# Six conditioning blocks of the second layer summed on ScalarE, GpSimd and VectorE for one column

## The chip, the cores and the metric

The kernel runs on one core of a Trainium2 chip. The metric is the device time of one execution in microseconds (us). Besides DMA the core has TensorE (PE in the rows; its weight loads are PEld), VectorE (DVE), ScalarE (ACT), GpSimd (POOL) and SyncE (SP), which here only issues DMAs. Each engine works through its own instructions in the order in which the program holds them.

## The reference, cut to what matters

Two layers of a trunk act on 256 latent and 256 context tokens of 1024 channels. Each layer is conditioned: a vector of 6 x 1024 numbers, for the latents and for the context apart, gives a shift, a scale and a gate to the token mixing and to the channel mixer.

```python
for l in range(DEPTH):                                  # DEPTH = 2
    last = l == DEPTH - 1
    mod = silu(c) @ w_mod[l] + b_mod[l]                 # (1024) x (1024, 6144)
    mod_c = silu(c_ctx) @ w_mod[l] + b_mod[l]
    sh1, sc1, g1, sh2, sc2, g2 = split(mod, 6)
    csh1, csc1, cg1, csh2, csc2, cg2 = split(mod_c, 6)
    h = modulate(rmsnorm(x, norm_mix[l]), sh1, sc1)
    hc = modulate(rmsnorm(xc, norm_mix[l]), csh1, csc1)
    mix, mix_c, v_pair = token_mixers(h, hc, ...)       # attention, RWKV-7, spatial gating
    x = x + g1 * mix
    h = modulate(rmsnorm(x, norm_ffn[l]), sh2, sc2)
    x = x + g2 * swiglu(h, w1, w3, w2)
    if not last:
        ...                                             # the same for the context, with cg1, csh2, csc2, cg2
return x                                                # the latents alone
```

In the last layer csh2, csc2 and cg2 are used by nothing.

## The kernel before

The work of a layer is: `phase_ab` (all projections of the token mixers, the recurrence, attention, spatial gating), `phase_m` (merge of the branches and output projection) and `phase_f` (channel mixer). Weights come in tiles of 128 x 1024 (512 KB) through SP into the tag `wr` (`wtile`, line 153), which in the second layer's `phase_ab` has three buffers. ScalarE rounds each half (`wh`, line 124), VectorE or, for the gates, GpSimd forms the rest (`wl`, line 125), and three products per 128 channels restore the precision. The results of all projections, of the conditioning and of its transposes share two PSUM buffers, the tag `mm`.

`phase_ab` is made of threads: K (projections of a pair of heads, `rps`), P (`psc`, `pvs`, `pbk`), I (inverse of triangular blocks, mostly on VectorE, `itp` and `it` at lines 629 and 630), C (the recurrence, `cw`, `cu`, `cn`, `py`), Q (its output norm), A and T (attention, `ptm`, `pt`, `po`), S (spatial gating), G (24 gate projections, `gps`, evicted by ScalarE into `gth` at line 362 and stored to `gate_d` at line 363) and X, the conditioning. `slots` sets the order in which their steps are emitted; a scheduler then puts the instructions of every engine in an order by priority and by when it takes buffers to be free. C, I and P have high priority, X and G have none.

The 12 conditioning blocks of a layer are 512 columns of `w_mod` each. `mod` computes a block for both columns (latents and context) on TensorE: the four quarters of 256 rows are loaded in turn (line 243, 512 KB each), and each quarter gives eight products of the 128 x 32 stationary `cr[:, k]` with 128 columns of weights into the PSUM tile `mps` (line 246).

```python
for k in range(2):
    for g in range(4):
        mm(ps[32*g:32*g+32], cr[:, 2*q+k], w[:, 512*k+128*g:512*k+128*g+128],
           start=q+k == 0, stop=q+k == 4)
```

So a block has 32 products and keeps its PSUM tile from the first to the copy in `spread`. `spread` (line 224) copies the rows to the SBUF tile `modr` on ScalarE (line 227), transposes it on TensorE (`mpt`, line 229), and VectorE adds the bias into `modv` (line 230). `mod_v` (line 252) does the same for both columns on the vector engines, and is used in the first layer's `phase_f`: products with a column of `cr` on VectorE and ScalarE (lines 264 to 270), sums on VectorE and GpSimd (`macc`, lines 266 and 271), and at the end products with the selectors `sel` that bring the sum over the partitions (`mvp`, line 276).

The blocks run as follows. First layer: 0 to 3 before `phase_ab`, 4 to 8 as thread X of `phase_ab`, 9 in `phase_m`, 10 and 11 by `mod_v` in `phase_f`. Second layer: 0 to 5 by `mod_v` in the first layer's `phase_f`, and 6 to 11 by `mod` as thread X of the second layer's `phase_ab` (`m1`, line 1142). Blocks 6 to 11 are the shift, scale and gate of the channel mixer; the results of `m1` are taken up after `phase_ab`.

Of the kernel before, what the change touches and what calls it, by code (L numbers as in the profile page):

```python
# [7 lines left out]
F32 = mybir.dt.float32  # L8
# [6 lines left out]
PSUM = bass.MemoryType.PSUM  # L15
# [30 lines left out]
def slots(p):  # L46
    """the order in which the stages of the time mixing are emitted: by a time given to each"""
# [38 lines left out]
def trunk(ctx: ExitStack, tc: tile.TileContext, out, a):  # L86
# [3 lines left out]
    def dm(cl, l, *args, **kw):  # L90
        """a product of a dense class: in the order of the program with the others of the classes in DENSE"""
        r = mm(*args, **kw)  # L92
        if cl in DENSE:
            tc.stamp_issue_order_token(r.ins, f"dense{l}")
        return r
# [31 lines left out]
    def rsqrt(pool, out, x, scale, bias, tag):  # L127
        """out = 1 / sqrt(scale * x + bias): a first guess from the bits, three steps of Newton's method"""
# [10 lines left out]
    class Wt:  # L139
        """a block of weights in two halves of 512 columns, each split into its two parts"""  # L140
# [27 lines left out]
    # conditioning  # L168
# [25 lines left out]
    def params2(L):  # L194
# [11 lines left out]
        # time-mixing vectors  # L206
# [17 lines left out]
    def spread(L, j, ps):  # L224
        """rows 32 g + i of ps to column i of the vectors of block j"""
        r = gp.tile([128, 128], F32, tag="modr", name="modr")
# [6 lines left out]
    def mod(L, js, pool=None, nb=2):  # L233
        """conditioning blocks of 512 columns, 128 to each group of 32 rows of the product; a generator that stops after every quarter of a block"""
# [17 lines left out]
    def mod_v(L, js, pool, share):  # L252
        """the same on the vector engines; a generator that stops after every quarter of a block"""
# [24 lines left out]

    def run(gen, n=None):
# [13 lines left out]
    class Norm:  # L293
        """of x [128, KT, 512], into hh and hl: the squares of each 128 channels, then the rest"""
# [51 lines left out]
    def proj(ps, w, ts_, kt=KT, cl=None, l=0):  # L346
        """feature-major: ps [128, n] = w^T h"""
# [17 lines left out]
    def phase_ab(L, extra):  # L365
        """the three branches up to what the merge takes, as threads whose stages are emitted in the order of slots()"""
# [6 lines left out]
        with tc.tile_pool(name="pb", bufs=1, reuse_waits="tile", side="right") as pb, tc.tile_pool(name="pe", bufs=1, reuse_waits="tile") as pe, tc.tile_pool(name="pbp", bufs=1, space=PSUM, reuse_waits="tile") as pbp:  # L373
# [16 lines left out]
            def conv(ps, w, y, streams):  # L390
                """y [128, ns*256] from ps, zero padded in each stream"""
# [14 lines left out]
            def rnorm(sq, n, scale, bias, name):  # L406
                """1/sqrt(scale * sum over the head + bias), token-major and spread over the head"""
# [12 lines left out]
            def rnorm2(rx, n, name):  # L420
                """the same, feature-major, in PSUM"""
# [14 lines left out]
            if last:  # L436
                # value residual: low rank part
# [24 lines left out]
            def t_common(hp):  # L462
                """one pair of heads: projections, removal key, rates, bonus"""
# [53 lines left out]
            def dirs(ap, d):  # L517
                """[128, 256] of one stream as [128, 4, 64] in the order of processing"""
# [717 lines left out]
```

## Time and profile before

| what | value |
|---|---|
| time, median of 3 runs | 2234.27 us |
| the three runs | 2232.68, 2237.18, 2234.27 us |
| profiled execution, from its first to its last instruction (its span; the page has no other time of it) | 2235.2 us |
| busy: PE, DVE, ACT, POOL | 93%, 60%, 38%, 22% of the span |
| TensorE clock granted, mean | 0.891 |
| second layer's `phase_ab`, its part with conditioning | 1420 to 1840 us |

A busy share counts time in which an engine has an instruction under way; matmuls are pipelined and their ends are modelled, so that a busy TensorE need not be a full one. The chain of work that ended last follows the program back from its last instruction, at each step to what released it: a microsecond on the chain is one that the end waited for. fp32 products appear as two records each.

### The profile page before, as it was taken

The page shows a single profiled execution, that of the slowest core. Times are in us where ns is not written, and L with a number is a line of the kernel's source. Part 1 is how long each engine was busy: PE and PEld are TensorE (multiplying, and loading weights), DVE is VectorE, ACT ScalarE, POOL GpSimd, SP SyncE. Part 2 cuts the span into 40 slices and gives each one's busy share as a digit, 9 for nine tenths or more (in the row PEclk, how much of TensorE's full clock was granted, in tenths as well). Part 3 has the DMA queues.
Part 4 walks back from the last instruction along what each step waited for, and adds up shares of the span by engine and source line. Part 5 has one row for each costly group of instructions (what it writes and reads, how often), then busy time and mean ns, then how long its engine had stood idle before and what let it go on. Part 6 is the DMA issues. An engine that isn't in the chain of part 4 may idle for free.

```text
span 2235.2 us, 36124 instructions
## 1 busy us (share of the span) xinstructions
PE 2075.2 (93%) x13738; PEld 1627.7 (73%) x13738; DVE 1332.0 (60%) x3383; ACT 856.1 (38%) x1776; POOL 498.1 (22%) x589
## 2 busy tenths in 40 slices
PE   4989999899999989898999988899999999988999
PEld 3867666566666668787888867776766667878999
DVE  3576568456367235576753356675876667177665
ACT  3442233443233432354342334432433344245554
POOL 3131132222222223032210002414241333330000
PEclk8997689987878999999999989785997888699999
DMA  7222113221111286245542222311212121375553
GB/s 259 86 72 72 57 34 101 71 69 41 54 44 37 68 319 197 86 150 165 175 145 95 78 90 85 96 58 48 82 61 70 61 88 59 99 256 174 186 181 114
DMA packets 97738, 239.24 MB, mean 107 GB/s; under 512 B 9594, under 2 KB 25594, under 8 KB 97436
## 3 DMA queue, kind: packets, MB, share of 16 engines
q1 hardware_dynamic: 90012, 225.39, 30.7%
q10 hardware_dynamic: 6912, 9.44, 1.2%
q8 instruction: 108, 1.77, 0.3%
q0 software_dynamic: 640, 2.10, 0.3%
q14 instruction: 66, 0.54, 0.1%
HBM read 219.59 MB, written 17.30 MB: 106 GB/s over the span
## 4 chain that ended last, share of the span: by engine, by line
PE 75%; DVE 12%; DMA 4%; issue 3%; ACT 3%; POOL 3%; SPq 0%; ACTq 0%; POOLq 0%; DVEq 0%
PE fps L92 16%; PE gps L92 8%; PE rps L92 6%; PE psc L579 3%; PE yps L1074 3%; PE yps L1075 3%; PE yps L1076 3%; PE mps L246 2%; PE sc L845 2%; DVE it L630 2%; PE pvs L590 2%; DMA mr<-in_w_mod 2%; PE cu L698 1%; DVE itp L629 1%; PE py L686 1%
## 5 line engine op out<-in xcount | busy, mean ns | idle before, releaser
L124 ACT CAST wh<-wr 128x512 fp32r<-128x512 f32 (+1 forms) x560 | 340.5, 613 | 539.5 <-PE fps L92 158.9
L125 DVE TENSOR_TENSOR wl<-wr,wh 128x512 fp32r<-128x512 f32 x464 | 332.4, 721 | 228.9 <-ACT wh L124 206.4
L92 PE MATMUL fps<-hh,wh 128*128 128x256 f32 (+1 forms) x720 | 240.7, 337 | 2.2 <-ACT hh L339 2.2
L92 PE MATMUL fps<-hl,wh 128*128 128x256 f32 (+1 forms) x720 | 240.5, 336 | 0.8 <-POOL hl L344 0.8
L92 PE MATMUL fps<-hh,wl 128*128 128x256 f32 (+1 forms) x720 | 240.8, 335 | 0.0
L125 POOL TENSOR_TENSOR wl<-wr,wh 128x512 fp32r<-128x512 f32 x96 | 126.7, 1323 | 310.6 <-ACT wh L124 182.4
L92 PE MATMUL gps<-hh,wh 128*128 128x512 f32 (+1 forms) x384 | 150.3, 391 | 4.2 <-ACT gth L362 3.6
L92 PEld LDWEIGHTS fps<-hh,wh 128*128 128x128 f32 x720 | 138.1, 193 | 16.7 <-ACT hh L339 3.0
L92 PE MATMUL gps<-hh,wl 128*128 128x512 f32 (+1 forms) x384 | 150.2, 391 | 0.0
L92 PE MATMUL gps<-hl,wh 128*128 128x512 f32 (+1 forms) x384 | 150.1, 391 | 0.0
L92 PEld LDWEIGHTS fps<-hl,wh 128*128 128x128 f32 x720 | 138.1, 192 | 14.3 <-POOL hl L344 1.2
L92 PEld LDWEIGHTS fps<-hh,wl 128*128 128x128 f32 x720 | 138.4, 192 | 12.9
L630 DVE TENSOR_TENSOR it<-it,itp 128x60 f32<-128x60 f32 (+24 forms) x496 | 130.0, 266 | 8.1
L629 DVE TENSOR_TENSOR itp<-it,ix 128x60 f32<-128x60 f32 (+24 forms) x496 | 124.4, 255 | 7.2
L92 PE MATMUL rps<-hh,wh 128*128 128x512 f32 (+1 forms) x224 | 101.0, 451 | 20.0 <-ACT hh L339 13.4
L1074 PE MATMUL yps<-fgh,wh 128*128 128x512 f32 (+1 forms) x352 | 119.2, 339 | 0.0
L1075 PE MATMUL yps<-fgl,wh 128*128 128x512 f32 (+1 forms) x352 | 119.0, 338 | 0.0
L1076 PE MATMUL yps<-fgh,wl 128*128 128x512 f32 (+1 forms) x352 | 118.8, 337 | 0.0
L579 PE MATMUL psc<-AR,BK 64*128 64x128 f32 (+1 forms) x512 | 85.0, 315 | 16.7 <-DVE BK L570 5.3
L92 PE MATMUL rps<-hl,wh 128*128 128x512 f32 (+1 forms) x224 | 98.9, 442 | 0.7 <-DVE hl L341 0.7
L92 PE MATMUL rps<-hh,wl 128*128 128x512 f32 (+1 forms) x224 | 97.8, 437 | 0.3 <-DVE wl L125 0.3
L579 PEld LDWEIGHTS psc<-AR,BK 64*128 64x128 f32 x512 | 73.1, 217 | 33.3 <-issue 10.7
(372 smaller groups left out, 4638.2 us busy)
## 6 DMA issues: line engine op xcount, KB each, us to landing
wr<-in_w SPq DMA_DIRECT2D x120, 512.0 KB, 3.5
wr<-in_w_fm SPq DMA_DIRECT2D x84, 512.0 KB, 3.5
mr<-in_w_mod SPq DMA_DIRECT2D x52, 512.0 KB, 4.4
wr<-in_w_mod SPq DMA_DIRECT2D x44, 512.0 KB, 3.7
wr<-in_w_o SPq DMA_DIRECT2D x24, 512.0 KB, 5.2
wr<-in_w_tm SPq DMA_DIRECT2D x20, 512.0 KB, 3.5
wr<-in_w_out SPq DMA_DIRECT2D x16, 512.0 KB, 4.6
gate_d<-gth ACTq DMA_DIRECT2D x24, 256.0 KB, 2.3
```

The lines of the kernel that those rows point to most:

```text
L92: r = mm(*args, **kw)
L124: S.copy(hi, raw)
L125: (eng or V).tensor_sub(lo, raw, hi.bitcast(F32))
L246: mm(ps[32 * g:32 * g + 32], cr[:, 2 * q + k], w[:, 512 * k + 128 * g:512 * k + 128 * g + 128], start=q + k == 0, stop=q + k == 4)
L579: mm(ps[:, c - c0, 0:64 * ns], BK[hs[x], c].rearrange("p a j -> p (a j)"), AR[hs[x], c, 0:ns].rearrange("p a j -> p (a j)"), start=True, s ...
L590: mm(ps[64:128, c], vd[0:64], ident[0:64, 0:64], start=True, stop=True)
L629: V.tensor_tensor(tv, Tm[:, t0:, s:s + 1].broadcast_to([128, n, s]), X[:, s, 0:s].unsqueeze(1).broadcast_to([128, n, s]), op=ALU.mult)
L630: V.tensor_tensor(Tm[:, t0:, 0:s], Tm[:, t0:, 0:s], tv, op=ALU.add)
L845: mm(sc, qT[p0:p0 + 64, pr, qs], kT[p0:p0 + 64, :kn], start=True, stop=qt < 2)
L1074: mm(ps[:, :n], wh, gh_[k][:, :n], start=k == 0, stop=False)
L1075: mm(ps[:, :n], wh, gl_[k][:, :n], start=False, stop=False)
L1076: mm(ps[:, :n], wl, gh_[k][:, :n], start=False, stop=k == nf - 1)
```

## The change

Blocks 6 to 11 of the second layer are computed by a new function `mod_1` in place of `mod`, for the latent column alone. Per quarter ScalarE multiplies the two halves of the weight tile by their columns of `cr`, in place; GpSimd adds the two; VectorE adds that to `macd` (for the first quarter GpSimd writes `macd` itself). Per block four products with `sel[:, 0]` remain on TensorE, then `spread` as before. The context column of these blocks then holds the bias alone. The step that ends a block runs with the first quarter of the next one. `spread` no longer has a tile tag of its own: in all its uses, those of the first layer too, its `modr` now takes a buffer of the tag `gth`, of which there are two and which the gates use.

```diff
     def spread(L, j, ps):
-        r = gp.tile([128, 128], F32, tag="modr", name="modr")
+        r = gp.tile([128, 512], F32, tag="gth", name="modr")[:, 0:128]
         S.copy(r, ps)
...
+    def mod_1(L, js):
+        for j in js:
+            acc = gp.tile([128, 512], F32, tag="macd", bufs=1, name="macd")
+            for q in range(4):
+                turn[0] += 1
+                ww = ([wp_] + more)[turn[0] % (1 + len(more))].tile([128, 1024], F32, tag="wr", bufs=WR, name="wr")
+                nc.sync.dma_start(ww, a["w_mod"][L.l][256 * q:256 * q + 256, 512 * j:512 * j + 512].rearrange("(k p) n -> p k n", p=128))
+                w0, w1 = ww[:, 0:512], ww[:, 512:1024]
+                S.mul(w0, w0, cr[:, 2 * q, 0:1])
+                S.mul(w1, w1, cr[:, 2 * q + 1, 0:1])
+                if q == 0:
+                    G.tensor_add(acc, w0, w1)
+                else:
+                    G.tensor_add(w0, w0, w1)
+                    V.tensor_add(acc, acc, w0)
+                yield
+            ps = pmm.tile([128, 128], F32, tag="mm", name="mvp")
+            for g in range(4):
+                mm(ps[32 * g:32 * g + 32], sel[:, 0], acc[:, 128 * g:128 * g + 128], start=True, stop=True)
+            spread(L, j, ps)
...
-                m1 = mod(L, range(NX, 12))
+                m1 = mod_1(L, range(NX, 12))
```

The rest of the diff takes comments and docstrings out. In the changed file the lines behind `mod_v` stand 22 lines further down (the gate's copy at 384 for 362, the recurrence's `cu` at 720 for 698).

On TensorE in the second layer's `phase_ab`, where the second block of the six begins, the order before is this (`mps` is the conditioning, `gps` a gate, `py`, `cn`, `cw` and `cu` the recurrence, `pa` a thread K):

```order
L698 MATMUL cu_13061<-cws_13052,TT_12967 64x64 x4
L92 MATMUL gps_13335<-hh_90,wh_13327 128x256
L92 MATMUL gps_13335<-hl_91,wh_13327 128x256
L246 MATMUL mps_13372<-wr_13373,cr_83 32x128
L714 MATMUL py_13045<-SC_12691,VS_12870 64x64 x2
L246 MATMUL mps_13372<-wr_13373,cr_83 32x128 x4
L705 MATMUL cn_13117<-VS_12870,BKT_13018 64x64 x4
```

and with the change this, from the same step of the recurrence on (`mvp` are the four products that close a block):

```order
L727 MATMUL cn_13104<-VS_12857,BKT_13005 64x64 x4
L736 MATMUL py_13032<-SC_12682,VS_12857 64x64 x2
L298 MATMUL mvp_13350<-macd_12197,sel_86 32x128 x4
L92 MATMUL gps_13313<-hh_90,wl_13306 128x256
L92 MATMUL gps_13313<-hh_90,wh_13305 128x256
```

The transpose of the same block stands here (`psc` is thread P):

```order
L601 MATMUL psc_13578<-AR_13473,BK_13476 128x64 x4
L736 MATMUL py_13032<-SC_12682,VS_12857 64x64 x2
L229 MATMUL mpt_13357<-cst_74,modr_13355 128x128
L92 MATMUL gps_13394<-hh_90,wh_13386 128x256
L727 MATMUL cn_13223<-VS_12857,BKT_13005 64x64 x4
```

The products of the conditioning that stood between the steps of the recurrence are gone; four products per block are left. Between them and the block's transpose stand 45 other rows, the rest of the gate `gps_13313` among them.

On VectorE in the same stretch, before (`gg` and `AR` are thread P, `sm` a thread K):

```order
L508 TENSOR_SCALAR sm_13316<-sm_13316,bo_11324 128x256
L486 TENSOR_TENSOR v_13068<-v_13068,vf_13107 128x512
L709 TENSOR_TENSOR VS_12870<-cn_13117,csp_13058 64x2x64 x2
L514 TENSOR_TENSOR bv_13323<-pbn_13321,v_13068 128x256
L568 TENSOR_TENSOR gg_13502<-gg_13502,kT_12511 64x512
L568 TENSOR_TENSOR gg_13523<-gg_13523,kk_13261 64x512
```

and with the change (`macd` is the new sum):

```order
L530 TENSOR_SCALAR sm_13294<-sm_13294,bo_11324 128x256
L294 TENSOR_TENSOR macd_13360<-macd_13360,wr_13366 128x512
L590 TENSOR_TENSOR gg_13477<-gg_13477,kT_12506 64x512
L294 TENSOR_TENSOR macd_13360<-macd_13360,wr_13433 128x512
L590 TENSOR_TENSOR gg_13489<-gg_13489,kk_13239 64x512
L579 TENSOR_TENSOR AR_13473<-kk_13239,Pp_13452 128x4x64 x2
```

A sum now stands ahead of each of two operand products of thread P; each sum waits for GpSimd's, and that for ScalarE's.

On ScalarE in the first layer's `phase_ab`, before, around the end of the third block of thread X (`modr` from `mps`):

```order
L683 COPY cws_3168<-cw_3163 128x128
L227 COPY modr_3526<-mps_2906 128x128
L699 COPY VS_2955<-cu_3174 64x2x64
L124 CAST wh_3784<-wr_3782 128x512
L683 COPY cws_3253<-cw_3248 128x128
```

and with the change, where the same copy now stands:

```order
L384 ACTIVATE gth_3505<-gps_3480 128x512
L721 COPY VS_3298<-cu_3680 64x2x64
L879 ACTIVATE ap_3344<-ap_3344,st_3237 128x256
L227 COPY modr_3526<-mps_2906 128x128
L385 DMA gate_d_77<-gth_3505 128x512
```

The copy moved behind two gates, `gth_3216` and `gth_3505`. So did the copies of the next two blocks, behind one gate (`gth_4017`) and two (`gth_4216`, `gth_4362`); up to the third copy the order of the first layer is as before.

## Rows read from the trace of the kernel before

**Rows 1.** The page's part 1: busy time, share of the span, instructions

```profile
PE 2075.2 (93%) x13738; PEld 1627.7 (73%) x13738; DVE 1332.0 (60%) x3383; ACT 856.1 (38%) x1776; POOL 498.1 (22%) x589
```

**Rows 2.** The page's part 4: the chain by engine, shares of the span

```profile
PE 75%; DVE 12%; DMA 4%; issue 3%; ACT 3%; POOL 3%; SPq 0%; ACTq 0%; POOLq 0%; DVEq 0%
```

**Rows 3.** Windows of the second layer: length, busy per engine, clock, DMA share, GB/s

```profile
1420.00:1840.00 420.00, 401.16 (x3025) 295.59 (x3023) 285.87 (x907) 157.59 (x348) 127.80 (x165) 0.80 0.21 69
...
1900.00:1945.00 45.00, 43.50 (x295) 36.10 (x293) 7.96 (x27) 10.05 (x26) 12.61 (x14) 0.59 0.15 49
```

**Rows 4.** The chain from 1420 to 1840 us: by line; a piece: start, us, what

```profile
by line: PE rps L92 12.1%; PE psc L579 7.7%; PE mps L246 6.1%; PE gps L92 6.0%; PE pvs L590 4.3%; DVE it L630 3.5%; PE cu L698 2.8%; PE pvs L591 2.8%; DVE itp L629 2.7%; PE cw L681 2.6%; PE pc L544 2.4%; PE sc L845 2.2%; PE po L873 2.2%; PE
...
1824.73 5.23 DMA wr<-in_w_mod
```

**Rows 5.** Windows, tile mps alone, 1420 to 1840 us: length, PE, PEld, ACT, clock

```profile
1420.00:1840.00 420.00, 35.77 (x384) 14.94 (x384) 1.61 (x6) 0.80 0.21 69
```

**Rows 6.** Tile macc (`mod_v`, first layer): duration ns min/median/max, first and last start

```profile
L276 PE MATMUL mvp<-macc,sel x128: 272/273/421, 984.6 to 1152.5; 128*32 128x128 f32 x128
...
L271 POOL TENSOR_TENSOR macc<-macc,mr x32: 1266/1470/3327, 965.3 to 1146.0; 128x512 f32<-128x512 f32 x32
...
L264 ACT ACTIVATE macc<-mr,cr x8: 720/726/729, 961.3 to 1130.3; 128x512 f32<-128x512 f32 x8
```

**Rows 7.** Line 312, a VectorE sum of two SBUF tiles (columns as in 6)

```profile
L312 DVE TENSOR_TENSOR nacc<-nacc,nsq x28: 417/692/859, 9.8 to 2033.8; 128x512 f32<-128x512 f32 x21, 128x256 f32<-128x256 f32 x7
```

**Rows 8.** Tile it, 1420 to 1840 us (columns as in 6)

```profile
L629 DVE TENSOR_TENSOR itp<-it,ix x212: 156/213/1481, 1450.3 to 1837.7; 128x60 f32<-128x60 f32 x9, 128x54 f32<-128x54 f32 x7, 128x31 f32<-128x31 f32 x6, 128x28 f32<-128x28 f32 x6
L630 DVE TENSOR_TENSOR it<-it,itp x212: 154/212/1701, 1450.5 to 1839.2; 128x60 f32<-128x60 f32 x9, 128x54 f32<-128x54 f32 x8, 128x31 f32<-128x31 f32 x6, 128x28 f32<-128x28 f32 x6
```

**Rows 9.** SyncE's waits, 1420 to 1840 us: us in total, times, longest

```profile
SPq L158 <- PE mps L246: 78.8, 14, 19.0
...
SPq L243 <- PE mps L246: 45.1, 8, 15.7
```

**Rows 10.** Timeline of ScalarE, first layer, three copies and the gates behind them

```profile
358.88 0.27 ACT L227 COPY modr<-mps 128x128 f32<-128x128 f32 x1 [0.32 <-PE mps L246]
...
394.01 0.60 ACT L362 ACTIVATE gth<-gps 128x512 f32<-128x512 f32 x1
...
424.13 0.26 ACT L227 COPY modr<-mps 128x128 f32<-128x128 f32 x1
450.21 0.59 ACT L362 ACTIVATE gth<-gps 128x512 f32<-128x512 f32 x1
...
486.31 0.27 ACT L227 COPY modr<-mps 128x128 f32<-128x128 f32 x1 [0.46 <-PE mps L246]
...
527.72 0.60 ACT L362 ACTIVATE gth<-gps 128x512 f32<-128x512 f32 x1 [0.46 <-PE gps L92]
```

**Rows 11.** The page's part 5: a gate's products; busy, mean ns | idle before, releaser

```profile
L92 PE MATMUL gps<-hh,wh 128*128 128x512 f32 (+1 forms) x384 | 150.3, 391 | 4.2 <-ACT gth L362 3.6
```

**Rows 12.** Costliest lines of VectorE, 1420 to 1840 us: busy us, mean ns | idle before

```profile
L629 DVE TENSOR_TENSOR itp<-it,ix 128x54 f32<-128x54 f32 (+23 forms) x212 | 52.5, 257 | 2.3
L630 DVE TENSOR_TENSOR it<-it,itp 128x54 f32<-128x54 f32 (+22 forms) x212 | 52.4, 258 | 2.3
```

**Rows 13.** Windows, tile mps alone, four stretches of 20 us (columns as in 5)

```profile
1500.00:1520.00 20.00, 0.00 (x0) 0.00 (x0) 0.00 (x0) 0.50 0.16 54
...
1540.00:1560.00 20.00, 5.33 (x40) 2.08 (x40) 0.00 (x0) 0.50 0.17 54
...
1620.00:1640.00 20.00, 4.29 (x32) 1.61 (x32) 0.27 (x1) 1.00 0.31 104
...
1720.00:1740.00 20.00, 0.00 (x0) 0.00 (x0) 0.00 (x0) 0.70 0.11 34
```

## The prediction

> **What bounds the kernel now.** I read the busy shares first, then the chain of waits, then the stretch in which the change lies. TensorE is busy for 93% of the span, VectorE for 60%, ScalarE for 38%, GpSimd for 22% [rows 1]; of the chain that ended last TensorE holds 75%, VectorE 12%, ScalarE and GpSimd 3% each [rows 2]. A microsecond taken from TensorE is thus likely to be seen at the end, and one added to another engine is not, or in small part. The six blocks run between 1420 and 1840 us. There TensorE is busy for 401.2 of 420 us and leaves 18.8 us; VectorE has work for 285.9, ScalarE for 157.6, GpSimd for 127.8 us [rows 3]. Behind it, between 1900 and 1945 us, TensorE is still busy for 43.5 of 45 us while VectorE works for 8 [rows 3]: the gates that are left share it with the last steps of the recurrence. Gates have no priority and fill what others leave, so TensorE time that is saved earlier lets them come earlier. In the chain of this stretch the conditioning products hold 6.1% [rows 4].
>
> **The change, part by part.** The sum is made against the span of the profiled execution, 2235.2 us. The median of the runs shown, 2234.27 us, is 0.9 us below it, so that what lies around the span is too small to see.
>
> *Products taken out.* 6 blocks x 32 products, 384 records, 35.8 us of busy TensorE [rows 5]. On the chain they hold 6.1% of 420 us = 25.6 us [rows 4], which is 0.72 of their busy time. I take 25.6; the ends are 14.9 us (their weight loads alone [rows 5]) and 35.8 us.
>
> *A load waited for.* Near the end of the stretch the chain runs through one conditioning load for 5.23 us [rows 4], with TensorE behind it. Its reader is now ScalarE, which has more room, but blocks others there. Ends 0 and 5.2; I take half, 2.6 us saved.
>
> *Products added.* 6 x 4 with the selector, 48 records. Their kind took as long as those taken out (median 273 ns of one, overlapped [rows 6]), so 35.77 / 384 = 93 ns each [rows 5], 4.5 us, of which 0.72 on the chain: +3.2 us. Six copies, transposes and bias additions stay.
>
> *ScalarE.* 48 products of 128 x 512 at 0.726 us [rows 6]: 34.8 us more. Of its 38% the chain holds 3% [rows 1, 2], so by that share 2.7 us. Ends: 0, if all lie in its gaps, and three times the share, since the copies of the recurrence queue behind them.
>
> *GpSimd.* 24 sums at 1.47 us [rows 6]: 35.3 us, by its share (3 of 22) 4.8 us; ends 0 and twice the share.
>
> *VectorE.* 18 sums of two SBUF tiles at 0.69 us [rows 7]: 12.4 us, by its share (12 of 60) 2.5 us. To that comes what GpSimd takes from it. The small operations of the inversion, at a median of 0.21 us, reach 1.70 us [rows 8]; so one may be held up for 1.5 us. If each of the 24 new GpSimd sums did this once it would be 35.8 us of VectorE, 7.2 on the chain; if none, nothing. I take half, 3.6 us. The Trainium skill (SBUF — State Buffer, "Who interferes with whom") says that a VectorE instruction with two SBUF inputs and a GpSimd instruction that reads SBUF exclude each other for a whole instruction. The longest inversion operation, as long as a GpSimd sum, agrees; that the median is far lower shows how seldom they meet now. By the rule the term is its upper end, 7.2 us, only if every new sum meets one.
>
> *Loads and buffers.* As many loads of the same size go through SyncE, in nearly the same places. Each now gives its buffer back after two ScalarE products and one or two sums (2 x 0.73 + 1.47 + 0.69 = 3.6 us) in place of 16 records at 93 ns (1.5 us). Queued behind it on SyncE are weight tiles and the stores of finished outputs. SyncE waits there for conditioning products to free a buffer for 78.8 and 45.1 us already [rows 9] with TensorE 95% busy, so the loads have slack: nothing, with an end of 5.2 us lost, another wait like the one above.
>
> *The shared tag.* In the first layer three copies of finished blocks move behind gates that in the trace ended 35.1, 26.1 and 41.4 us later [rows 10]. For these 103 us the block keeps one of the two PSUM buffers for results. All waits of a gate's first products for an eviction into `gth` come to 3.6 us in the whole kernel [rows 11]. I take +1.0 us, ends 0 and 3.6. In the second layer the four products' tile is held for some 45 rows per block; before, the accumulator was held for the whole block. That can only give room; I take nothing, at most the idle 18.8 us.
>
> Sum: -25.6 - 2.6 + 3.2 + 2.7 + 4.8 + 2.5 + 3.6 + 1.0 = -10.4 us, so 2224.8, **2225 us**.
>
> **What the rows on TensorE leave open.** From 1420 to 1840 us its weight loads are busy for 295.6 of 420 us, 70%, against 95% for products [rows 3]; if the rest of the 95% is waiting in a pipeline, products taken out give back less than they show. This is the first rival.
>
> **Rivals.**
>
> 1. *TensorE is less full than it looks.* The products taken out then give their weight loads' 14.9 us alone [rows 5]: -14.9 - 2.6 + 17.8 = +0.3, 2235.5 us, no change. For it: the 70%. Against: the conditioning products stand on the chain with 25.6 us, many in small groups between steps of the recurrence. The Trainium skill (Perfetto Trace Analysis, "Identifying the Most-Contended Engine") says that matmul busy time is no good measure of how full TensorE is and that the share of weight loads is a better one. By that rule the sum is this rival's; no row decides between them. Chance 0.16.
>
> 2. *VectorE's inversions become the bound.* The 424 inversion operations of the stretch take 52.5 + 52.4 us [rows 12] one after another, and the recurrence waits for them. The new load on VectorE is at most 35.8 + 12.4 = 48.2 us, of which the sum has 6.1. Without these 6.1 the sum is -16.5; once more than 16.5 us of the 48.2, a third, lie on the path the change loses, and at 60% (28.9 us) the time is 2247.6 us. For it: operations of up to 1.70 us [rows 8], and sums that stand in VectorE's queue ahead of thread P while they wait for GpSimd and ScalarE. Against: 134 us without work on VectorE in the stretch [rows 3]. Chance 0.14.
>
> 3. *The other engines hide it all.* Then the loss is 3.2 us and the gain 28.2: -25.0, 2210.2 us. For it: ScalarE and GpSimd have work for under 40% of the stretch [rows 3], and a PSUM buffer is freed. Against: in-order queues in which new work stands ahead of the recurrence's copies. Chance 0.24.
>
> 4. *The clock falls.* The mean granted clock of the stretch is 0.80 [rows 3], a mixture of 2.4 and 1.2 GHz. Of four stretches of 20 us, one with 32 records had 1.00, one with 40 had 0.50, two without any had 0.50 and 0.70 [rows 13]. If the mean fell to 0.77, 401.2 x (0.80 / 0.77 - 1) = 15.6 us come on top: 2240.4 us, slower. The Trainium skill (TensorE: Matmul & The Clock Gate, "What's actually happening") says that the clock is held down unless activity releases it; by that rule the time moves towards this rival. The stretch with 40 records at 0.50 speaks against it. Chance 0.08.
>
> That the change does not do what it says I leave out: the last layer reads the latent column of these blocks alone.
>
> **How the numbers follow.** The forecast has 0.38, its own range 2217 to 2232. About 0.2% (4.5 us) is what a measurement of this kernel can tell from no change. Faster by more: rival 3 and most of the forecast, 0.24 + 0.34 = 0.58. Within it: rival 1 and the forecast's upper end, 0.16 + 0.04 = 0.20. Slower: rivals 2 and 4, 0.22. The range reaches below rival 3, by 4 us for more of the idle TensorE time, to 2206, and above rival 4, for a smaller case of rival 2 (25 us on the path, -16.5 + 25 = +8.5), to 2244.
>
> **What would show it.** In the profile after: no `mps` from 1420 us on, 48 `mvp` records; TensorE's busy time lower by about 31 us (35.8 - 4.5); TensorE still over 90% busy in the second `phase_ab`; the stretch up to the merge shorter by about 10 us. The first layer up to 815 us should be within 4 us of before. If TensorE's busy time fell by 31 us and the time did not, rival 1 or 2 holds: idle time in front of weight loads would show the first, longer `it` and `itp` rows and TensorE waits that VectorE ends the second. A granted clock below 0.78 over the stretch shows the fourth. The prediction is wrong if the first layer moves more than the second, or if the new sums end more than 10 us of TensorE's waits.

## The result and the profile after

The changed kernel takes 2283.45 us (median of 4; 2279.38 to 2296.09) against 2235.72 us in the same comparison. The medians lie 47.7 us apart, 2.1%; the ratio on record for the comparison, which is not the quotient of these two medians, is 1.031, 95% interval 1.023 to 1.039. By either the change is **slower by 2 to 3%**; 2225 us, faster, had been forecast. Single executions of one kernel spread by over 1% here, and the ratios below leave out those that lie more than 1.5% above the fastest of their kernel, while the medians are over all of them.

The busy shares and the chain by engine of the kernel after, in the columns of [rows 1] and [rows 2]:

```profile
PE 2087.7 (92%) x13402; PEld 1649.9 (72%) x13402; DVE 1369.5 (60%) x3401; ACT 885.9 (39%) x1824; POOL 530.4 (23%) x613
...
PE 74%; DVE 14%; DMA 4%; issue 3%; ACT 3%; POOL 2%; SPq 0%; DVEq 0%; POOLq 0%; ACTq 0%
```

336 records of products are gone, and yet TensorE's busy time has gone up by 12.5 us where the forecast had it fall by 31. Its idle time, span less busy time, went from 160.0 to 190.5 us. The two differences, 12.5 and 30.5, are the 43.0 us by which the span grew (2278.2 against 2235.2). Work that shrinks and takes longer points to the clock, so the windows come next. After (length, busy per engine, clock, DMA share, GB/s):

```profile
0.00:1420.00 1420.00, 1303.64 (x7773) 988.80 (x7774) 810.86 (x1978) 522.44 (x1073) 309.97 (x361) 0.91 0.32 106
1420.00:1940.00 520.00, 473.62 (x3204) 363.86 (x3202) 364.40 (x1045) 214.49 (x461) 190.21 (x219) 0.74 0.21 67
1940.00:2190.00 250.00, 225.58 (x1724) 212.57 (x1723) 144.39 (x292) 110.86 (x219) 30.19 (x34) 0.87 0.53 169
...
1420.00:1840.00 420.00, 376.70 (x2439) 289.91 (x2437) 299.34 (x839) 174.42 (x365) 159.86 (x185) 0.73 0.23 72
```

The first three stretches of the kernel before:

```profile
0.00:1420.00 1420.00, 1305.52 (x7788) 986.24 (x7789) 812.41 (x1979) 523.42 (x1074) 309.24 (x361) 0.91 0.32 106
1420.00:1940.00 520.00, 494.34 (x3730) 370.01 (x3729) 336.07 (x1068) 189.71 (x426) 156.56 (x198) 0.79 0.20 65
1940.00:2190.00 250.00, 233.47 (x1878) 229.80 (x1877) 160.76 (x294) 125.62 (x242) 32.31 (x32) 0.97 0.61 203
```

Up to 1420 us the two agree to 3 us on every engine and in the clock. From there TensorE has less work under way (473.6 for 494.3 us) at a lower granted clock (0.74 for 0.79); in the six blocks' own stretch it idles for 43.3 us, for 18.8 before [rows 3], at 0.73. The third stretch holds more of the recurrence after than before. Cut where the recurrence ends (its last `cn` begins at 1925 us before and at 1976 after), the windows are, before:

```profile
1420.00:1925.00 505.00, 479.34 (x3638) 357.06 (x3638) 333.33 (x1056) 185.46 (x416) 152.70 (x194) 0.79 0.20 66
...
1960.00:2231.00 271.00, 256.08 (x2072) 252.92 (x2071) 173.70 (x321) 133.25 (x256) 17.66 (x20) 0.97 0.56 183
```

and after:

```profile
1420.00:1976.00 556.00, 507.44 (x3452) 391.28 (x3450) 374.97 (x1075) 222.80 (x481) 198.74 (x228) 0.73 0.21 67
...
2005.00:2275.00 270.00, 258.90 (x2070) 254.57 (x2070) 173.38 (x321) 132.48 (x253) 16.82 (x20) 0.97 0.55 174
```

So the whole loss arises before the recurrence ends: 51 us more there, 8 us less from there to the end. The output projection and the channel mixer, the second window of each pair, run as before, at 0.97. The recurrence's score products show the clock as a duration; their rows before and after, 1420 to 1940 us (ns min/median/max):

```profile
L579 PE MATMUL psc<-AR,BK x256: 272/272/580, 1431.2 to 1857.2; 64*128 64x64 f32 x64, 64*128 64x128 f32 x64
```

```profile
L601 PE MATMUL psc<-AR,BK x256: 272/417/579, 1433.4 to 1906.8; 64*128 64x64 f32 x64, 64*128 64x128 f32 x64
```

The same 256 records; the middle one takes 417 ns for 272, and the last starts 50 us later. The clock falls in many places of the stretch, before too [rows 13]. One of them can be followed on the chain of the kernel after (start, us, what); its longest piece from 1420 to 1940 us, shown first, is one of VectorE's new sums, which have a median of 0.68 us:

```profile
1558.26 3.73 DVE macd L294
...
1610.83 0.35 PE gns L433 x4
...
1611.37 3.42 DVE itp L651
...
1616.39 1.16 PE psc L601 x8
...
1619.02 2.00 PE psc L601 x8
...
1623.66 2.00 PE psc L601 x8
```

At 1611 us an inversion operation of VectorE lies on the chain with 3.42 us; its like has a median of 0.21 us. Behind it eight score products take 1.16 us, and from 1619 us on 2.00. TensorE's windows of the kernel after (length, busy, clock, DMA, GB/s) tell what it did before that:

```profile
1611.00:1616.00 5.00, 2.14 (x10) 1.00 0.00 0
1616.00:1636.00 20.00, 19.61 (x74) 0.56 0.28 92
```

For 5 us it was busy for 2.1 at 1.00, the 2.4 GHz level; the next 20 us it was busy throughout at a mean of 0.56, nearly all at 1.2 GHz. What ran while VectorE was held up is in GpSimd's timeline:

```profile
1610.92 1.34 POOL L590 TENSOR_TENSOR gg<-gg,kT 64x512 f32<-64x512 f32 x1 [8.74 <-ACT gg L587]
1612.22 1.27 POOL L125 TENSOR_TENSOR wl<-wr,wh 128x512 fp32r<-128x512 f32 x1
1613.46 1.25 POOL L293 TENSOR_TENSOR wr<-wr 128x512 f32<-128x512 f32 x1
```

and in VectorE's:

```profile
1611.29 3.50 DVE L651 TENSOR_TENSOR itp<-it,ix 128x54 f32<-128x54 f32 x1
```

The operation begins 0.4 us after the first of three GpSimd instructions and ends (1614.79) with the last (1614.71), which is one of the new sums. The Trainium skill (SBUF — State Buffer, "Who interferes with whom") says that a VectorE instruction with two SBUF inputs contends with a GpSimd instruction that reads SBUF, and that the ports they share are held exclusively. The trace agrees and goes further: the wait lasted through a run of GpSimd instructions. The longest inversion operations of f2 and f3 below, 3.66 and 3.67 us, also lie beside three such instructions in a row. The prediction had priced one sum per hit.

So the inversions took longer: 304 and 302 ns for one operation against 258 and 257 [rows 12], and the longest 3502 ns against 1701 [rows 8].

```profile
L652 DVE TENSOR_TENSOR it<-it,itp 128x60 f32<-128x60 f32 (+24 forms) x186 | 55.2, 304 | 2.2
L651 DVE TENSOR_TENSOR itp<-it,ix 128x66 f32<-128x66 f32 (+24 forms) x186 | 55.0, 302 | 1.9
```

Over the whole second layer, 1420 to 2000 us, count times mean of the two rows comes to 129 us before and to 149 after:

```profile
L629 DVE TENSOR_TENSOR itp<-it,ix 128x60 f32<-128x60 f32 (+23 forms) x248 | 63.4, 264 | 2.9
L630 DVE TENSOR_TENSOR it<-it,itp 128x54 f32<-128x54 f32 (+22 forms) x248 | 61.7, 257 | 3.1
```

```profile
L651 DVE TENSOR_TENSOR itp<-it,ix 128x60 f32<-128x60 f32 (+24 forms) x248 | 74.3, 305 | 3.2
L652 DVE TENSOR_TENSOR it<-it,itp 128x60 f32<-128x60 f32 (+24 forms) x248 | 72.4, 297 | 3.8
```

The eight inversions start (transposes of `ild` into `ix`) at 1448, 1469, 1576, 1608, 1686, 1723, 1807 and 1860 us before, and 2, 5, 5, 29, 35, 56, 37 and 50 us later after.

### The profile page after: what moved, and what is told of

Read it like the earlier page. It is cut to its first block, busy times and chain, and to the rows that moved or that the text cites. A ratio compares the mean times of both kernels' runs of the same rounds, so it can differ in the third digit from the quotient of the medians.

```text
span 2278.2 us, 35578 instructions
## 1 busy us (share of the span) xinstructions
PE 2087.7 (92%) x13402; PEld 1649.9 (72%) x13402; DVE 1369.5 (60%) x3401; ACT 885.9 (39%) x1824; POOL 530.4 (23%) x613
## 4 chain that ended last, share of the span: by engine, by line
PE 74%; DVE 14%; DMA 4%; issue 3%; ACT 3%; POOL 2%; SPq 0%; DVEq 0%; POOLq 0%; ACTq 0%
PE fps L92 16%; PE gps L92 8%; PE rps L92 6%; PE psc L601 3%; PE yps L1098 3%; PE yps L1097 3%; PE yps L1096 3%; DVE it L652 2%; DVE itp L651 2%; PE sc L867 2%; PE pvs L612 2%; DMA mr<-in_w_mod 1%; PE cw L703 1%; PE py L708 1%; PE cu L720 1%
## 5 line engine op out<-in xcount | busy, mean ns | idle before, releaser
L92 PE MATMUL gps<-hh,wh 128*128 128x512 f32 (+1 forms) x384 | 161.0, 419 | 4.1 <-ACT gth L384 3.6
L92 PE MATMUL gps<-hl,wh 128*128 128x512 f32 (+1 forms) x384 | 158.2, 412 | 0.0
L92 PE MATMUL gps<-hh,wl 128*128 128x512 f32 (+1 forms) x384 | 156.7, 408 | 0.0
L652 DVE TENSOR_TENSOR it<-it,itp 128x60 f32<-128x60 f32 (+24 forms) x496 | 140.6, 286 | 8.4
L651 DVE TENSOR_TENSOR itp<-it,ix 128x60 f32<-128x60 f32 (+24 forms) x496 | 135.9, 276 | 7.7
L601 PEld LDWEIGHTS psc<-AR,BK 64*128 64x128 f32 x512 | 82.0, 239 | 34.2 <-issue 12.6
L601 PE MATMUL psc<-AR,BK 64*128 64x128 f32 (+1 forms) x512 | 93.9, 338 | 13.6 <-DVE AR L581 4.5
L92 PEld LDWEIGHTS gps<-hh,wh 128*128 128x128 f32 x384 | 88.6, 231 | 21.0 <-issue 4.8
L92 PEld LDWEIGHTS gps<-hh,wl 128*128 128x128 f32 x384 | 87.5, 228 | 14.9 <-issue 5.1
```

The costliest lines, as they stand in the source:

```text
L601: mm(ps[:, c - c0, 0:64 * ns], BK[hs[x], c].rearrange("p a j -> p (a j)"), AR[hs[x], c, 0:ns].rearrange("p a j -> p (a j)"), start=True, s ...
L651: V.tensor_tensor(tv, Tm[:, t0:, s:s + 1].broadcast_to([128, n, s]), X[:, s, 0:s].unsqueeze(1).broadcast_to([128, n, s]), op=ALU.mult)
L652: V.tensor_tensor(Tm[:, t0:, 0:s], Tm[:, t0:, 0:s], tv, op=ALU.add)
```

## Time and clock in 263 executions

Each execution comes with its time and its mean granted clock. In the 23 runs of the kernel before beside the kernel with sums of 8 columns, one program with one order of rows, times go from 2196.5 us at 0.914 to 2263.7 at 0.878. A straight line for each kernel with one common slope fits all 263 executions of the study to 3.9 us (rms): **0.01 of mean clock is worth 18.6 us**. That is what the chain gives: 75% of 2235 us is TensorE [rows 2], and 0.75 x 2235 x 0.01 / 0.89 = 18.8. With the slope each kernel's time can be read at one clock, 0.890; what is left to its own clock is the difference to its median.

| kernel | median us (runs) | ratio to before, interval | median clock | us at 0.890 |
|---|---|---|---|---|
| before (five comparisons) | 2230 to 2241 (105) | 1 | 0.889 to 0.897 | 2240 to 2242 |
| the change | 2283.5 (4) | 1.031, 1.023–1.039 | 0.868 | 2244 |
| e1 products back | 2251.0 (10) | 1.002, 0.997–1.006 | 0.887 | 2244 |
| e2 own buffer | 2267.3 (4) | 1.015, 1.009–1.021 | 0.878 | 2244 |
| e3 no sums | 2203.6 (4) | 0.979, 0.971–0.988 | 0.900 | 2218 |
| e4 change + idle products | 2260.6 (10) | 1.006, 1.002–1.011 | 0.893 | 2264 |
| f1 sums of 8 columns | 2207.4 (12) | 0.995, 0.990–0.999 | 0.899 | 2222 |
| f2 VectorE alone | 2261.9 (6) | 1.024, 1.014–1.033 | 0.881 | 2247 |
| f3 no VectorE sums | 2276.6 (6) | 1.028, 1.019–1.038 | 0.877 | 2253 |
| f4 ScalarE alone | 2218.8 (12) | 1.002, 0.994–1.009 | 0.894 | 2227 |
| g1 before, order moved | 2236.4 (12) | 0.998, 0.994–1.002 | 0.894 | 2243 |
| g2 before + idle products | 2267.5 (6) | 1.015, 1.009–1.021 | 0.898 | 2282 |
| g3 steps of 12 us | 2242.0 (12) | 1.008, 1.002–1.013 | 0.887 | 2235 |
| h1 in the channel mixer | 2231.4 (12) | 0.995, 0.991–1.000 | 0.892 | 2235 |
| k1 own buffer, 12 us | 2278.9 (6) | 1.014, 1.006–1.022 | 0.876 | 2248 |
| k2 steps of 10 us | 2284.1 (6) | 1.024, 1.019–1.028 | 0.873 | 2253 |
| k3 before, 12 us | 2293.3 (6) | 1.027, 1.022–1.033 | 0.876 | 2266 |
| k4 steps of 16 us | 2257.7 (6) | 1.013, 1.007–1.019 | 0.884 | 2245 |
| l1 mixer, own buffer | 2223.0 (12) | 1.001, 0.998–1.004 | 0.896 | 2234 |
| l2 no sums, 12 us | 2223.9 (12) | 0.997, 0.992–1.001 | 0.895 | 2232 |

Read at one clock the change stands 2 to 4 us above the kernel before. 0.025 of clock, from some 0.893 to 0.868, makes the other 46 of the 48 us.

The two profiled executions give nearly the same without the line. As an estimate, TensorE's work is its busy time times the mean clock: 2075.2 x 0.891 = 1849 us before and 2087.7 x 0.872 = 1820 after. At 0.891 the work after would keep it busy for 2043 us. So the products that are gone give back 32 us (31 had been forecast), 30.5 us of new idle time take that away again, and the lower clock costs 44.5.

## The experiments

Theory A: the sums delay the inversions, by VectorE's queue and by GpSimd shutting VectorE out; the recurrence comes late, TensorE gets gaps, and its clock falls. Rivals: the in-order queues and waits of the new rows, whatever they last (B); the missing products (prediction, rival 4); the shared buffer; a chance order of the rows. Every edit also gives the rows a new order, so a single kernel against another tells little here; the section on other orders below takes them together. e3, f1, f4 and l2 leave out results, as the edits and expectations say.

**Parts undone.** e1 to e4 ran together.

```diff
 e1 -m1 = mod_1(L, range(NX, 12))       +m1 = mod(L, range(NX, 12))
 e2 -r = gp.tile(..., tag="gth", ...)   +r = gp.tile(..., tag="macd", bufs=1, ...)
 e3 all S.mul, G.tensor_add, V.tensor_add of mod_1 out; sel times `ones`
 e4 + per quarter: mm(pd[32*g:32*g+32], cr[:, 2*q+k], cst[:, 128*g:128*g+128])  for k, g
```

Expected of e1:

> The conditioning of the second layer goes back to TensorE (both columns); the shared tag stays. Before has 2235, the change 2280 us. If the shared tag (with the order that it makes) costs the time, this stays near the change: over 2260 us. If the cost comes with the work on ScalarE, GpSimd and VectorE, or from the clock that falls without the products, this is at before: 2230 to 2242 us, with the granted clock from 1420 to 1840 us back at 0.80.

Of e2:

> The change, but the copy in spread takes the one buffer of the new sum in place of a buffer of the gates, so that no block waits for a gate. If the shared tag costs the time: below 2245 us. If the vector work or the clock does: 2270 to 2285 us, as the change.

Of e3:

> The change without its work on ScalarE, GpSimd and VectorE: the six blocks' weights are loaded and read by nothing, and the four closing products take a constant. The conditioning of these blocks is left out. If the vector work costs the time, what is left is the gain on TensorE alone: 2205 to 2222 us (before less 13 to 30). If the clock falls because the products are missing, it falls here too: over 2250 us, with a granted clock of about 0.73 from 1420 to 1840 us. If the shared tag does it: over 2255 us.

Of e4:

> The change, and beside it 32 products per block on TensorE as before, of constant tiles, whose result nobody reads. If the clock costs the time, they bring it back: 2235 to 2255 us, faster than the change, with a clock near 0.80. If the vector work does, they only add TensorE time: 2280 to 2310 us.

With the products back, 2251 us; without the sums, 2204 us. So the products' removal by itself gains, and the sums lose more than that. e1 is level with before by its ratio (1.002), but missed what was expected of it: its median lies above 2242 us, and the clock of the stretch came back to 0.75, not 0.80. At one clock e3 is 22 us below before, what the prediction had for the products (25.6 less 3.2); by the medians the clock is not lower without either (0.900 for 0.892 in its comparison). That takes the reason from rival 4: missing products don't starve the clock. The window of e3's profiled execution, which with a mean clock of 0.891 is the lowest of its four, stands between those of before and the change (columns as above):

```profile
1420.00:1940.00 520.00, 485.66 (x3534) 373.69 (x3533) 345.95 (x1080) 197.50 (x446) 170.80 (x206) 0.78 0.23 75
```

e4 is the odd one: 192 idle products more, 384 records, make the change faster by 23 us, between its two cases. At one clock they cost 20 us, and the clock rises from 0.868 to 0.893. The own buffer gave 16 us, between its two cases as well, and all of it by the clock (2244 us at one clock for both).

**Which part of the sums.** f1 to f4 ran together.

```diff
 f1 every S.mul, G.tensor_add, V.tensor_add on [:, 0:8]
 f2 -S.mul, G.tensor_add, V.tensor_add
    +V.tensor_scalar(acc, w0, cr[:, 0, 0:1], ...), then 7 x V.scalar_tensor_tensor(acc, wk, cr[:, 2*q+k, 0:1], acc, ...)
 f3 -V.tensor_add(acc, acc, w0)         +G.tensor_add(acc, acc, w0)
 f4 -if q == 0: ... else: ...           +acc = w1
```

Expected of f1:

> The change with every product and sum of the six blocks cut from 512 to 8 columns; instruction counts, loads, buffers and waits stay. It leaves out the sums of the other 504 columns, and the closing products read those 8 columns 16 times over. Theory A (the time that the 90 vector instructions take on ScalarE, GpSimd and VectorE, and the VectorE operations that GpSimd's sums hold up, delay the steps of the inversion and the recurrence): close to the kernel without any of them, 2195 to 2220 us, and the inversion's operations fall back to 124 and 130 us in the kernel. Theory B (what costs is the places and waits of these instructions in the in-order queues, whatever they last): 2255 to 2290 us, near the change's 2283.

Of f2:

> The change with all products and sums on VectorE, 8 multiply-and-add instructions of 128 x 512 per block, 48 in all at about 0.69 us = 33 us more on VectorE, nothing on ScalarE and GpSimd. Theory A as collisions with GpSimd: the loss becomes that of 33 us at VectorE's share, about 2204 + 33 x 0.2 to 0.5 = 2210 to 2225 us, and no inversion operation lasts over 1.8 us. Theory A as VectorE's own fullness, or theory B: 2250 to 2290 us.

Of f3:

> The change with VectorE's 18 sums moved to GpSimd: 42 sums there of about 1.3 to 1.5 us, 60 us in all; ScalarE's 48 products stay. If collisions with GpSimd's sums are what costs: 18 more of them, so no faster than the change, 2280 to 2305 us. If VectorE's own sums, which wait for GpSimd at the head of its queue, are what costs: 2215 to 2250 us.

Of f4:

> The change with ScalarE's 48 products alone: all sums are left out, and the closing products read one product of the last quarter. If ScalarE's part of the loss is by its share of the chain, as predicted: 2204 + 3 = 2200 to 2215 us. If ScalarE's queue is what delays the recurrence's copies: 2240 us or more.

f1 speaks for A and against B: with every instruction, load, buffer and wait there but 8 columns wide, 2207 us. It does not decide alone, since its order differs too: the order in which the traces show TensorE's rows differs between f1 and the change by 2,170 lines of a text comparison, between before and g1 below by 1,720. The inversions of its second layer fall back to 132 us in total (149 in the change, 129 before). No inversion operation of that layer exceeds 1.47 us:

```profile
L651 DVE TENSOR_TENSOR itp<-it,ix x217: 142/214/1464, 1451.5 to 1818.9; 128x60 f32<-128x60 f32 x9, 128x54 f32<-128x54 f32 x8, 128x31 f32<-128x31 f32 x6, 128x29 f32<-128x29 f32 x6
```

f4: ScalarE's 35 us alone cost 4 to 5 us at one clock, near the 2.7 of the prediction, but less than orders differ by. f2 and f3 missed their better cases: VectorE alone, without any new GpSimd sum, is nearly as bad as the change (42 instructions at a median of 746 ns), and so is GpSimd with 42 sums. f2's inversion operations still reach 3.66 us, beside GpSimd work that was there before. The longest operation by itself is no sign of a loss, though: h1 below, without a sum in the second layer, has one of 3.08 us there, and k2, as slow as the change, none over 1.48 there. The total is the better sign: 145 us in f2 and 159 in f3. It does not matter which of the two engines is loaded: each holds up the inversions.

**Place, order, filler.** h1 and g1 to g3 ran together.

```diff
 h1 -ww = ([wp_] + more)[...].tile(..., tag="wr", ...)   +ww = pool.tile(..., tag="mr", bufs=2, ...)
    +yield from mod_1(N, range(NX, 12), px)   in sf(), behind mod_v(N, range(NX), px, 2)
    -m1 = mod_1(L, range(NX, 12))             +m1 = iter(())
 g1 before: -'X': 32.2                        +'X': 34.2
 g2 before: + idle products of e4 in the second layer's mod, 384 records
 g3 -'X': 32.2, 'x': 8                        +'X': 32.2, 'x': 12
```

Expected of h1:

> The same sums of the six blocks, for the latents alone, made while the first layer's channel mixer runs (behind the eight blocks that it makes on the vector engines already), and none in the second layer. In the kernel before, TensorE is busy for 100 of 100 us at a granted clock of 1.00 from 1200 to 1300 us, with VectorE at 38, ScalarE at 29 and GpSimd at 0 us. Theory A (the sums cost because they delay the inversions and the recurrence, which leaves gaps on TensorE and a lower clock there): here they delay nothing, so as fast as the kernel without them, 2195 to 2220 us. Rival (90 more instructions on the vector engines cost wherever they stand, since they share queues with the casts of TensorE's weights): the mixer grows by 20 us or more and the time is 2230 us or more.

Of g1:

> The kernel before with one number changed: the second layer's conditioning blocks start 2 us later in the table that sets the order (34.2 in place of 32.2). No work is added or removed, about 1,770 of TensorE's rows change places (3,920 do in the change). If the loss of the change came from a chance order of the rows: 2250 us or more, or 2215 or less. If order of that kind is worth little: 2225 to 2242 us.

Of g2:

> The kernel before with 32 idle products more per block of the second layer on TensorE (64 in place of 32; nobody reads their result). At equal granted clock 384 idle products cost about 20 us in the change. If more products raise TensorE's clock wherever they stand: the clock rises from 0.892 to 0.905 or more and the time stays within 2230 to 2245 us. If they only fill gaps that the sums of the change had opened, and there are few such gaps before: the clock stays at 0.892 and the time is 2250 to 2265 us.

Of g3:

> The change with its quarter blocks 12 us apart in the table of the order in place of 8: the same sums, spread over a stretch half as long again. If what costs is that sums stand too closely among the inversions: 2255 to 2270 us. If each sum costs wherever it stands in the second layer's time mixing: 2275 to 2295 us.

h1 puts the same instructions where TensorE is saturated at a clock of 1.00, and the loss is gone: 52 us below the change, level with before or 0.5% below it. It fell short of theory A's 2195 to 2220 us and lies at the foot of the rival's case, for the sums are not free there either: the mixer's products (`fps`, `yps`), 379 us from first to last before, take 392. That is less than the rival's 20 us. Part of it is 7.3 us of TensorE waits in the mixer for copies of finished blocks:

```profile
PE mpt L229 <- ACT modr L227: 7.3, 5, 3.7
```

g1 met its case of little worth, 2236 us. g2 costs 42 us at one clock and raises the mean clock by 0.001 to 0.009 only (0.898 against 0.889 to 0.897), though in the six blocks' stretch of its profiled execution it is 0.85 against 0.80. Together with e4: idle products gained beside the sums, and lost without them. That they pay by filling gaps is not shown. The Trainium skill (TensorE: Matmul & The Clock Gate, "What's actually happening") says that the array is throttled unless activity releases it. The fall followed above (2.1 of 5 us busy, then 0.56) agrees; over longer stretches busy time does not settle the clock: from 1420 to 1940 us f1 was busy for 475.2 us at 0.84, the change for 473.6 at 0.74. g3 came out best of all with sums in the second layer, 41 us below the change, below both of its cases, and looked like less collision.

**Is it the spacing?** k1 to k4 ran together, with `'x'` at 12 on e2, at 10 on the change, at 12 on the kernel before and at 16 on the change.

Expected of k1:

> The change with both: the copy of a finished block in a buffer of its own, and quarter blocks 12 us apart in the table of the order. If the two costs are separate, their gains add: 2242 - 16 = 2220 to 2232 us, faster than the kernel before. If the wider steps already take away what the shared buffer costs: 2236 to 2248 us.

Of k2:

> The change with its quarter blocks 10 us apart, between the change's 8 (2283 us) and 12 (2242 us). If spreading the sums is what gives back the loss: 2252 to 2274 us, between the two. If 12 is one lucky order among many: anywhere, and at 2280 us or above as likely as below.

Of k3:

> The kernel before with its quarter blocks 12 us apart; no sums on the vector engines. If wider steps help because the sums of the change then collide less with the inversions: no gain here, 2228 to 2246 us. If wider steps help whatever the blocks are computed with (they leave TensorE's filler for the end of the recurrence): 2200 to 2222 us, and then the change is still slower than products with the same steps.

Of k4:

> The change with its quarter blocks 16 us apart, so that the last two blocks come when the recurrence has ended (about 1930 us on). If the sums cost by delaying the inversions: less of them fall among the inversions, 2215 to 2240 us. If the late blocks make the merge wait: 2245 us or more, with waits of TensorE for the last blocks' copies.

It is not. By steps of 8, 10, 12 and 16 us the change takes 2283, 2284, 2242 and 2258 us, no line, and steps of 12 with the own buffer, each of which had gained, take 2279. k1 and k3 thus missed both of their cases, k2 met its second; k4 came into its worse case, but TensorE's waits for the copies of finished blocks, 5.5 us in its whole kernel for 2.8 before, do not explain that. The kernel before with steps of 12, not an instruction added, takes 2293 us: 60 us more than before from its order alone, as much as the whole result. It shares two signs with the change, a clock of 0.73 and late inversions (the eighth begins at 1912 us; 1909 in the change, 1860 before). It lacks the others: its inversions take 130 us in total, 129 before, and TensorE idles for 32.3 of 520 us, 25.7 before and 46.4 in the change:

```profile
1420.00:1940.00 520.00, 487.73 (x3355) 356.51 (x3354) 314.90 (x996) 173.12 (x388) 141.69 (x175) 0.73 0.18 61
```

**What the sums cost in other orders, and the better version.** l1 is h1 with the copy in `macd` and the sums in `macc`, l2 is e3 with `'x'` at 12.

Expected of l1:

> The six blocks' sums in the first layer's channel mixer as before (2231 us, TensorE waited there 7.3 us for copies of finished blocks), with those copies in a buffer of their own. If the shared buffer made these waits: they go, and the time is 2215 to 2228 us. If the copies were late because ScalarE was busy: no change, 2228 to 2236 us.

Of l2:

> The kernel without the sums (it leaves out the products and sums of the six blocks and reads constants) with quarter blocks 12 us apart. At a mean clock of 0.89 the kernel without sums stood at 2218 us and five orders of the change at 2235 to 2253 us. If the sums themselves cost those 25 us: 2210 to 2226 us at that clock here too. If the order alone makes such differences (12 us steps cost the kernel before 60 us): 2235 us or more at that clock.

l2 lies between its two cases, at 2232 us for 0.890. Kernels without full sums in the second layer stand at 2218, 2222 and 2232 us there (e3, f1, l2), six orders of the change at 2235 to 2253, mean 2245 (the change, e2, g3, k1, k2, k4). So the sums cost 21 us at one clock, with some 7 us either way from the order, and the clock of their kernels is lower by 0.020 (0.877 against 0.898 in the mean): 38 us more. The first link of theory A shows in every order tried: the inversions of the second layer take 141 to 159 us in the nine kernels with full sums beside them, and 123 to 137 us in the eleven others. So does the second, on the whole: the eighth inversion begins by 1864 us in ten kernels, with medians of 2204 to 2258 us, and from 1879 us on in the ten others, with 2251 to 2293. But the first does not always bring the second (g3 and k4 have sums and are not late), and an order can bring the second alone (k3). Theory A holds for the kind; the size of a single order doesn't follow from it.

All this sets sums against no sums. Sums against products is another matter: six orders of the change take 2242 to 2284 us, 2269 in the mean, four with products (before, g1, e1, k3) 2235 to 2293, 2254 in the mean, and with steps of 12 the change (g3) is 51 us faster than the products (k3). How much of the 48 us belongs to sums in place of products and how much to this pair of orders, these runs do not tell.

l1 kept its waits (6.2 us), though its median lies in the first of its cases, and is level with before (1.001); its mixer takes 395 us. The sums in the channel mixer thus beat the change by over 2%, and before by 0.5% in one of two forms, by nothing in the other: a version that clearly beats both was not found.

## Why the prediction was wrong

- **What failed is the step that left the clock out of the sum.** It stood at 0, and as rival 4 at 15.6 us with a chance of 0.08. Read at one clock, it made 46 of the 48 us. The price was too small because 0.77 was taken and 0.73 came; with that, rival 4's own formula gives 401.2 x (0.80 / 0.73 - 1) = 38.5 us. The reason was the wrong one too: without the products and without the sums the clock did not fall (e3, l2), with the sums' full time it did (0.877 against 0.898 in the mean), and in k3 it fell without any sum, by the order alone (0.876). That the sums do it through gaps on TensorE is argued, not shown.
- **Products out, -25.6, and in, +3.2:** at one clock -22 us in e3, -18 in f1, -8 in l2. The size was about right, the upper half of what was found against before; l2 against k3, both with steps of 12, gives -34. The weight loads' 14.9 us (rival 1) lie in the same span; these runs do not tell the two apart.
- **ScalarE +2.7:** 4 to 5 us (f4 against f1), within what orders differ by.
- **GpSimd 4.8, VectorE 2.5, held up 3.6, together 10.9:** 17 us at one clock (the change against f4), 21 over all orders with ScalarE's part. By shares of the chain alone this was too low: the inversions take 20 us more in total in the change, and in 1420 to 1840 us `it` and `itp` rose from 6.2% [rows 4] to 13.3% of the chain:

```profile
by line: PE gps L92 9.8%; PE rps L92 9.5%; PE psc L601 9.1%; DVE itp L651 6.7%; DVE it L652 6.6%; PE pvs L612 3.9%; PE pc L566 2.5%; PE pvs L613 2.4%; issue 2.4%; PE cw L703 2.2%; DVE macd L294 2.0%; PE sc L867 1.9%; PE pa L523 1.9%; PE pbk
```

- **The load, -2.6:** no load is among the five longest pieces of the chain from 1420 to 1940 us any more; the 5.2 us are gone, and cannot be seen beside the rest.
- **Shared tag, +1.0:** 16 us lost with steps of 8, 37 gained with steps of 12 (e2, k1). By the ratios the two are 36 and 15 us. That is order, and no price for the tag comes out of it. The prediction's 35.1, 26.1 and 41.4 us run from start to start of copy and gate, not to the gate's end.
- **Rival 2** had the mechanism, VectorE's inversions as the bound, and gave 2247.6 us, close to the 2244 at one clock. It lacked what came with the clock. Rivals 2 and 4 were held apart as alternatives, 0.14 and 0.08; here both came together.
- **The signs named:** the first layer unchanged and 48 `mvp` held. TensorE's -31 us of busy time did not come (+12.5), and a clock below 0.78 did. New sums end no wait of TensorE in the list; they act through VectorE's queue, so that sign was badly chosen.
- **The range,** 2206 to 2244, had no term for a new order of thousands of rows; k3 shows that one such order is worth 60 us. The 0.2% that it took a measurement to tell apart was too fine as well: the intervals above reach 0.3 to 1.0% to either side.

Open: why one order keeps the clock and the next loses it. g1 moved 1,770 of TensorE's rows for nothing, k3 lost 60 us. In profiled executions, TensorE's idle time from 1340 to 1940 us does not sort the kernels by clock (64 us at 0.84 in l1, 45 us at 0.76 in k3). Where the gaps lie may matter; no run here isolates that. That the fall at 1616 us was caused by the gap at 1611 is read from one trace, not tried by itself.

## What to carry to other kernels

Before you move work off a busy TensorE, find the serial path that feeds it and price the new work there, at its own duration and with what it shuts out, not at an engine's share of the whole chain. Put such work where TensorE is saturated and waits for nobody rather than beside a recurrence, and price it there too: in h1 it made the mixer 13 us longer. Take time and granted clock of many executions together: read at one clock, a loss of 48 us fell apart into a wash in work and 0.025 of clock, and a change of nothing but the order (k3) should be run as a control before any gain or loss is put down to an edit.

## What had not been expected

- 0.01 of mean granted clock is worth 18.6 us of this kernel, and the same program ran at 0.878 and at 0.914.
- An operation of 0.21 us took 3.50 us while three GpSimd instructions ran one after another.
- 192 products that nobody reads made the change faster by 23 us, and the kernel before slower by 26 to 33.
- The output projection and the channel mixer behind the recurrence run as before; all of the loss arises ahead of them.
- A step of 12 for 8 us in the order's table cost the kernel before 2.7% and gave the change 1.8% back.
